# Attention scores of a hybrid encoder block: the keys' low parts by head in full-height tiles, three pools with less in them

## The chip, the cores and the metric

The kernel is one program on one core of a Trainium2 chip. It holds a whole encoder layer, so the attention that is changed here is one stage among several. The metric is the device time of one execution in microseconds (us), the median of several. Engines are named as the profile names them: PE is the TensorE matmul, PEld its weight load, DVE the vector engine, ACT the scalar engine, POOL GpSimd, SP the queue that issues most DMAs.

## The reference, cut to what matters

Mixer B of the layer is attention in chunks of 64 frames: the queries of a chunk see their own chunk and the eight before it, with a bias by clipped distance. There are 8 heads of 64 channels and 1024 frames.

```python
def one_chunk(c):
    qc = q[c*64 : c*64 + 64]                # 64 queries
    kc, vc = kp[...], vp[...]               # 576 keys and values: own chunk and 8 before
    s = einsum('bqhd,bkhd->bhqk', qc, kc) * dh ** -0.5 + bias
    s = where(valid, s, -inf)
    p = softmax(s, axis=-1)
    return einsum('bhqk,bkhd->bqhd', p, vc)
```

Ahead of it stand the RMSNorm, one input projection and mixer A (a gated delta rule); behind it the branch projections with their gates, the output projection, and a feed-forward part with a short convolution.

## The kernel before, in words

**Split operands.** Matmuls run on float32r operands, and precision is kept by splitting a float32 operand into a high part (a rounded copy, made on ACT) and a low part (the rest, a subtraction on DVE or POOL). A product takes two or three matmuls: high by high, low by high, high by low.

**Stages.** In the trace mixer A runs to about 457 us; then come four pairs of attention heads, to about 757 us, then the branch and output projections and the feed-forward part. This case is about the four pairs.

**A pair.** `att_qkv` computes the operands of a pair in half-rows of 512 frames: `proj_half` does 24 matmuls of 512 columns into a PSUM tile `psph` (pool `psP`, two buffers), `scaled` multiplies it by the row scale into `u` on DVE (three buffers), and from `u` come Q, K and V. For head j of the pair, `Q[j]` holds 128 rows: the 64 rows of its own head are the high part of the queries, the other 64 their low part. `Kh[j]` holds the high part of the keys twice, in both halves, so that one matmul of 128 rows gives (query high + query low) by key high. `Kl`, the keys' low part, is one tile for both heads, 64 rows for each. The half-rows of V stay in `u` until `v_half` transposes them on PE into `psvt`.

**A head.** `att_head` goes through 8 query tiles of 128 frames. `scores(t)` makes two products into a PSUM tile `pss` (two buffers):

```python
mm(pss[:, o + s0:o + s1], q, Kh[:, ks], start=True, stop=False)
mm(pss[:, o + s0:o + s1], q[own], Kl[own, ks], start=False, stop=True)
```

The first takes all 128 rows, the second the 64 rows of the head. The band is up to 640 keys, written as pieces of 384 and 256 columns: a tile with t of 4 or more has two pieces and so four matmuls, the four tiles before have one piece (256, 256, 384, 512) and two matmuls. That makes 8 heads x (4 x 4 + 4 x 2) = 192 matmuls, 96 of either product, in 64 score tiles. DVE then adds the bias and takes the row maximum in one pass into `Sb` (four buffers), ACT takes the exponential, DVE scales; `weighted(t)` transposes `Sb` on PE into `psp` and splits it into `PTh` and `PTl`; `values` multiplies them with V into `pso` for every second tile, and the two halves of `pso` are added into `obT` by way of a tile `cor`.

**Order.** `weave` interleaves the turns of `att_pair` (scores run two tiles ahead of their transposes) with the steps of `att_qkv` for the next pair, or with gate projections in the last pair. The tile scheduler then sets the order on each engine by its own estimate, pool buffers included; each engine runs its list in order. So fewer buffers change the order of the program as well as the waits.

Of the kernel before, what the change touches and what calls it, by code (L numbers as in the profile page):

```python
# [8 lines left out]
F32 = mybir.dt.float32  # L9
F32R = mybir.dt.float32r  # L10
AF = mybir.ActivationFunctionType
ALU = mybir.AluOpType
# [4 lines left out]
P = 128  # L17
D = 1024
KT = D // P
T = 1024  # L20
NT = T // P
HN = 512
# [20 lines left out]
BAND = 640  # L43
# [3 lines left out]
def hybrid_kernel(ctx: ExitStack, tc: tile.TileContext, a):  # L47
    nc = tc.nc
    last = {}

    def mm(*args, **kw):
        last["mm"] = nc.tensor.matmul(*args, **kw).ins  # L52
# [591 lines left out]
    c, steps = gdn_qkv(0, ws, lambda e: psc.tile([P, HN], F32, tag="c", name="psph"))  # L644
# [7 lines left out]
    for h in range(-1, GH):  # L652
# [29 lines left out]
        if more:  # L682
            c, steps = gdn_qkv(h + 2)
# [43 lines left out]
    obT = obp2.tile([P, 4, T], F32, name="obT")  # L727
    ax = ExitStack()
    ap_ = ax.enter_context(tc.tile_pool(name="ap", bufs=1, reuse_waits="tile"))
    aq1 = ax.enter_context(tc.tile_pool(name="aq1", bufs=1, reuse_waits="tile"))  # L730
    aqx = ExitStack()
    aq0 = aqx.enter_context(tc.tile_pool(name="aq0", bufs=1, side="right", reuse_waits="tile"))
# [8 lines left out]

    W0 = 4 * GH

    def att_qkv(pr, c):
        c["pr"] = pr
        aq = (aq0, aq1)[pr % 2]
        Q = [aq.tile([P, T], F32R, tag=f"Q{j}", name=f"Q{j}") for j in range(2)]
        Kh = [aq.tile([P, T], F32R, tag=f"Kh{j}", name=f"Kh{j}") for j in range(2)]
        Kl = aq.tile([P, T], F32R, tag="Kl", name="Kl")
        V = aq.tile([P, NT, 256], F32R, tag="V", name="V")  # L750
        Vb = V.bitcast(F32)
        vT = [None, None]

        def scaled(w, e):

            ps, s = proj_half(w, BH, BL, KT, e)
            u = ap_.tile([P, HN], F32, tag="u", name="u", bufs=3)
            nc.vector.tensor_mul(u, ps, rb[:, s])
            return u, s

        def q_half(w, e):
            ps, s = scaled(w, e)
            for j in range(2):
                r = slice(j * 64, (j + 1) * 64)
                x = slice((1 - j) * 64, (2 - j) * 64)
                nc.scalar.activation(Q[j][r, s], ps[r], AF.Copy, scale=0.125)
                nc.vector.scalar_tensor_tensor(out=Q[j][x, s], in0=ps[r], scalar=0.125, in1=Q[j].bitcast(F32)[r, s],
                                               op0=ALU.mult, op1=ALU.subtract)

        def k_half(w, e):  # L770
            ps, s = scaled(w, e)
            for j in range(2):
                r = slice(j * 64, (j + 1) * 64)
                x = slice((1 - j) * 64, (2 - j) * 64)
                nc.scalar.copy(Kh[j][r, s], ps[r])
                nc.scalar.copy(Kh[j][x, s], ps[r])
                nc.vector.tensor_tensor(out=Kl[r, s], in0=ps[r], in1=Kh[j].bitcast(F32)[r, s], op=ALU.subtract)

        def v_half(e):
            ps = psP.tile([P, HN], F32, tag="p", name="psvt")  # L780
            for t in range(4):
                nc.tensor.transpose(out=ps[:, t * P:(t + 1) * P], in_=vT[e][:, t * P:(t + 1) * P],
                                    identity=ident)
            pv = ps.rearrange("p (n j d) -> p n j d", j=2, d=64)
            n = slice(4 * e, 4 * e + 4)
            for j in range(2):
                nc.scalar.copy(V[:, n, j * 192:j * 192 + 64], pv[:, :, j, :])
                nc.vector.tensor_tensor(out=V[:, n, 64 + j * 64:128 + j * 64], in0=pv[:, :, j, :],
                                        in1=Vb[:, n, j * 192:j * 192 + 64], op=ALU.subtract)

        w = load_w(a["w_tiles"][W0 + 8 + pr])
        for e in range(2):
            vT[e], s = scaled(w, e)
            yield
        wq = load_w(a["w_tiles"][W0 + pr])
        wk = load_w(a["w_tiles"][W0 + 4 + pr])
        c.update(Q=Q, Kh=Kh, Kl=Kl, V=V)
        q_half(wq, 0)
        yield
        v_half(0)  # L800
        k_half(wk, 0)
        yield
        v_half(1)
        q_half(wq, 1)
        yield
        k_half(wk, 1)
        yield

    def att_head(c, j):
        pr = c["pr"]  # L810
        h = 2 * pr + j
        Q, Kh, Kl, V = c["Q"][j], c["Kh"][j], c["Kl"], c["V"]
        own = slice(j * 64, (j + 1) * 64)
        bias = ap_.tile([P, BAND], F32, tag="bias", name="bias", bufs=2)
        nc.sync.dma_start(bias, a["rel"][h])
        nc.vector.memset(bias[64:128, 0:64], NEG)
        nc.vector.memset(bias[0:64, BAND - 64:BAND], NEG)

        def scores(t):
            nk = min(t + 1, 5)  # L820
            k0 = t + 1 - nk
            n = nk * P
            o = P if nk == 5 else 0
            pss = psS.tile([P, T], F32, tag="s", name="pss")
            pieces = ((0, 384), (384, 640)) if nk == 5 else ((0, max(n, 256)),)
            q = Q[:, t * P:(t + 1) * P]
            for s0, s1 in pieces:
                ks = slice(k0 * P + s0, k0 * P + s1)
                mm(pss[:, o + s0:o + s1], q, Kh[:, ks], start=True, stop=False)
            for s0, s1 in pieces:  # L830
                ks = slice(k0 * P + s0, k0 * P + s1)
                mm(pss[:, o + s0:o + s1], q[own], Kl[own, ks], start=False, stop=True)
            Sb = ap_.tile([P, BAND], F32, tag="Sb", name="Sb", bufs=4)
            st_ = sml.tile([P, 4], F32, tag="ast", name="ast")
            nc.vector.tensor_tensor_reduce(out=Sb[:, 0:n], in0=pss[:, o:o + n], in1=bias[:, BAND - n:BAND],
                                           scale=1.0, scalar=0.0, op0=ALU.add, op1=ALU.max,
                                           accum_out=st_[:, 0:1])
            nc.vector.tensor_scalar_mul(st_[:, 1:2], st_[:, 0:1], -1.0)
            nc.scalar.activation(Sb[:, 0:n], Sb[:, 0:n], AF.Exp, bias=st_[:, 1:2], accum_out=st_[:, 2:3])
            nc.vector.reciprocal(st_[:, 3:4], st_[:, 2:3])  # L840
            nc.vector.tensor_scalar_mul(Sb[:, 0:n], Sb[:, 0:n], st_[:, 3:4])
            return Sb, nk, k0

        def weighted(t, Sb, nk, k0):
            gq, e = t // 2, t % 2
            ph, pl = PT[gq % 2]
            es = slice(e * P, (e + 1) * P)
            for i0 in range(0, nk, 3):
                m = min(3, nk - i0)
                psp = psT.tile([P, 384], F32, tag="t", name="psp")  # L850
                for i in range(m):
                    nc.tensor.transpose(out=psp[:, i * P:(i + 1) * P], in_=Sb[:, (i0 + i) * P:(i0 + i + 1) * P],  # L852
                                        identity=ident)
                s0 = k0 + i0 - (2 * gq - 4)
                pv = psp[:, 0:m * P].rearrange("p (n q) -> p n q", q=P)
                nc.scalar.copy(ph[:, s0:s0 + m, es], pv)
                nc.vector.tensor_tensor(out=pl[:, s0:s0 + m, es], in0=pv, in1=ph.bitcast(F32)[:, s0:s0 + m, es],
                                        op=ALU.subtract)
        def values(gq):
            ph, pl = PT[gq % 2]  # L860
            f = 6 - min(2 * gq + 2, 6)
            pso = psT.tile([P, 256], F32, tag="t", name="pso")
            for s in range(f, 6):
                v = V[:, 2 * gq - 4 + s, j * P:(j + 1) * P]
                mm(pso, v, ph[:, s, :], start=s == f, stop=False)
                mm(pso, v, pl[:, s, :], start=False, stop=s == 5)
            cor = ap_.tile([P, 256], F32, tag="cor", name="cor")
            oth = slice((1 - j) * 64, (2 - j) * 64)
            nc.scalar.copy(cor[own], pso[oth])
            nc.vector.tensor_add(obT[own, pr, gq * 256:(gq + 1) * 256], pso[own], cor[own])  # L870

        for t in range(NT):
            yield lambda t=t: scores(t), lambda x, t=t: weighted(t, *x), (lambda t=t: values(t // 2)) if t % 2 else None
# [34 lines left out]
    c = {}  # L908
    for _ in att_qkv(0, c):
        pass  # L910
    for pr in range(4):
# [8 lines left out]
        c = nxt  # L920
# [23 lines left out]
    for o in range(KT):  # L944
        wa = load_w(a["w_ba_t"][o])
        wb_ = load_w(a["w_bb_t"][o])
        for e in range(2):
# [4 lines left out]
            ps, s = proj_half(wa, oh, ol, 4, e)  # L952
            nc.vector.scalar_tensor_tensor(out=ta, in0=ta, scalar=1.0, in1=ps, op0=ALU.add, op1=ALU.mult)
            ps, s = proj_half(wb_, bh, bl, 4, e)
# [192 lines left out]
    V, S, G, Q = Pinned(nc.vector), Pinned(nc.scalar), Pinned(nc.gpsimd), Pinned(nc.sync)  # L1147
# [127 lines left out]
    for i, t in enumerate(order):  # L1275
        if t == order[-1]:
            norm_b = norm_operands(order[i - 1], xt, wst, "hi", True)
            next(norm_b)
            o = up_load(0)
# [33 lines left out]
    s, c = slice(T - P, T), slice(HN - P, HN)  # L1313
# [47 lines left out]
    p, r = prs  # L1361
# [429 lines left out]
```

## Time and profile before

| | |
|---|---|
| median of 3 runs | 1605.38 us (1604.98 to 1606.62) |
| profiled execution | 1603.48 us, span of its instructions 1601.4 us |
| PE busy | 1561.8 us, 98% of the span |
| PEld, DVE, ACT, POOL busy | 78%, 70%, 43%, 37% |
| stage of the four pairs, 485 to 757 us | PE 269.35 of 272 us, DVE 194.88 us |

A busy share on PE says that some matmul was under way, not that it was at its pace: matmuls are pipelined, and in the rows below a matmul of 512 columns takes 0.39 us from start to end while the next one starts 0.23 us after it. What a matmul costs is therefore read as the distance from its start to the next start. In the timeline, rows of one kind that follow each other are merged ("x2"), with the start of the first. The column in square brackets is the idle time of the engine ahead of the row and what ended it; "issue" means that the profile shows no one who was waited for.

### The profile page before, as it was taken

To read this page: it belongs to the slowest core of one execution; us is meant where nothing else is said; L and a number is where in the kernel's file an instruction comes from. 1 tells how busy PE (TensorE), PEld (TensorE's weight loads), DVE (VectorE), ACT (ScalarE), POOL (GpSimd) and SP (SyncE) were. 2 spreads that over 40 slices of the span, in tenths; PEclk is the share of its full clock that TensorE was granted. 3 is DMA by queue.
4 is the path that set the end of the run, shared out by engine and by line. 5 is a ranking of instruction groups with operands and counts; after the bars stand their busy time and mean duration, and the time that the engine had idled before them with its cause. 6 is when DMAs were issued, how large, how long until landed. Compare 5 with 4: busy or idle time off the path is not lost.

```text
span 1601.4 us, 21106 instructions
## 1 busy us (share of the span) xinstructions
PE 1561.8 (98%) x7687; PEld 1254.7 (78%) x7687; DVE 1123.8 (70%) x2150; ACT 695.8 (43%) x1376; POOL 589.4 (37%) x445
## 2 busy tenths in 40 slices
PE   8999999999999999999999999999999999999997
PEld 6777776877777777778887887888888888788885
DVE  6795867948436867865665567677777777787787
ACT  7535333352224645554322335444444444333344
POOL 2422212212021101011220248877777776232352
PEclk9999999999999999999999999999999999999998
DMA  7021121122131101111654222233333322775523
GB/s 292 27 81 53 53 73 44 56 61 82 44 122 49 35 23 35 43 53 61 204 171 152 85 93 83 68 111 117 114 114 113 99 99 73 238 247 172 176 92 138
DMA packets 74503, 162.02 MB, mean 101 GB/s; under 512 B 15648, under 2 KB 16928, under 8 KB 74400
## 3 DMA queue, kind: packets, MB, share of 16 engines
q1 hardware_dynamic: 74400, 160.68, 30.2%
q8 instruction: 60, 0.98, 0.3%
q14 instruction: 43, 0.35, 0.1%
HBM read 120.55 MB, written 40.11 MB: 100 GB/s over the span
## 4 chain that ended last, share of the span: by engine, by line
PE 78%; DVE 7%; ACT 2%; issue 1%; DMA 1%; SPq 0%; POOL 0%; POOLq 0%; DVEq 0%; ACTq 0%
PE psph L52 27%; PE psd L52 7%; PE pb L52 7%; PE psout L52 5%; PE pc L52 5%; PE pa L52 4%; PE pb L1131 3%; PE pss L52 3%; PE psd L1483 3%; PE pso L52 3%; PE pc L1131 2%; PE pa L1131 2%; PE psp L852 2%; PE psws L52 1%; DVE tmp L506 1%
## 5 line engine op out<-in xcount | busy, mean ns | idle before, releaser
L82 POOL TENSOR_TENSOR wlo<-wraw,whi 128x1024 fp32r<-128x1024 f32 (+1 forms) x57 | 119.9, 2104 | 481.1 <-ACT whi L81 446.0
L52 PE MATMUL psph<-BH,whi 128*128 128x512 f32 x688 | 281.5, 409 | 9.7 <-ACT BH L220 5.2
L52 PE MATMUL psph<-BL,whi 128*128 128x512 f32 x688 | 278.2, 404 | 0.0
L52 PE MATMUL psph<-BH,wlo 128*128 128x512 f32 x688 | 275.9, 401 | 1.7 <-POOL wlo L82 1.7
L52 PEld LDWEIGHTS psph<-BH,whi 128*128 128x128 f32 x688 | 130.5, 190 | 37.0 <-ACT BH L220 5.9
L1145 POOL TENSOR_TENSOR ol<-wraw,oh 128x512 fp32r<-128x512 f32 x110 | 150.6, 1386 | 9.1 <-ACT oh L1145 9.1
L52 PEld LDWEIGHTS psph<-BH,wlo 128*128 128x128 f32 x688 | 130.5, 190 | 26.5 <-POOL wlo L82 2.1
L52 PEld LDWEIGHTS psph<-BL,whi 128*128 128x128 f32 x688 | 130.3, 189 | 24.5 <-DVE BL L221 1.5
L52 PE MATMUL psd<-wdl,ah 128*128 128x512 f32 (+1 forms) x311 | 121.8, 392 | 5.5 <-DVE wdl L1145 5.5
L1145 POOL TENSOR_TENSOR al<-araw,ah 128x1024 fp32r<-128x1024 f32 (+1 forms) x28 | 68.5, 2447 | 145.3 <-ACT ah L1145 145.2
L1145 POOL TENSOR_TENSOR wraw<-wraw 128x512 f32<-128x512 f32 x86 | 119.4, 1389 | 4.9
L1483 PE MATMUL psd<-wdh,al 128*128 128x512 f32 (+1 forms) x311 | 120.9, 389 | 0.0
L52 PE MATMUL psd<-wdh,ah 128*128 128x512 f32 (+1 forms) x311 | 119.8, 389 | 0.0
L1145 ACT CAST oh<-wraw 128x512 fp32r<-128x512 f32 x110 | 67.6, 619 | 102.0 <-POOL wraw L1145 101.9
L1145 DVE TENSOR_TENSOR wdl<-W,wdh 128x512 fp32r<-128x512 f32 x77 | 88.4, 1186 | 29.4 <-ACT wdh L1145 29.3
L1145 ACT CAST ah<-araw 128x1024 fp32r<-128x1024 f32 (+1 forms) x39 | 40.6, 1040 | 116.7 <-issue 51.9
L81 ACT CAST whi<-wraw 128x1024 fp32r<-128x1024 f32 (+2 forms) x61 | 55.2, 905 | 78.1 <-PE psph L52 54.9
L1145 POOL TENSOR_TENSOR gl<-wraw,gh 128x512 fp32r<-128x512 f32 x42 | 55.8, 1330 | 69.6 <-ACT gh L1145 69.6
L52 PEld LDWEIGHTS psd<-wdl,ah 128*128 128x128 f32 x311 | 58.8, 189 | 20.1 <-DVE wdl L1145 8.1
L1131 PE MATMUL pa<-BH,gh 128*128 128x512 f32 x176 | 68.6, 390 | 0.0
L52 PE MATMUL pa<-BL,gh 128*128 128x512 f32 x176 | 68.5, 389 | 0.0
L52 PE MATMUL pa<-BH,gl 128*128 128x512 f32 x176 | 68.5, 389 | 0.0
(341 smaller groups left out, 3826.1 us busy)
## 6 DMA issues: line engine op xcount, KB each, us to landing
wraw<-w_up SPq DMA_DIRECT2D x44, 512.0 KB, 5.0
wraw<-w_tiles SPq DMA_DIRECT2D x42, 512.0 KB, 3.5
araw<-dA SPq DMA_DIRECT2D x77, 256.0 KB, 3.0
dA<-yu SPq DMA_DIRECT2D x33, 512.0 KB, 3.1
W<-w_down SPq DMA_DIRECT2D x44, 256.0 KB, 4.8
xt<-x SPq DMA_DIRECT2D x16, 512.0 KB, 5.3
dG<-gt SPq DMA_DIRECT2D x16, 512.0 KB, 2.7
ta<-dG SPq DMA_DIRECT2D x16, 256.0 KB, 2.8
```

What stands on the lines that cost most here:

```text
L52: last["mm"] = nc.tensor.matmul(*args, **kw).ins
L81: nc.scalar.copy(hi, src)
L82: (eng or nc.gpsimd).tensor_tensor(out=lo, in0=src, in1=hi.bitcast(F32), op=ALU.subtract)
L506: nc.vector.tensor_tensor(out=tmp[:, :, 0:i], in0=Zt[:, :, 0:i], in1=Lr[:, i:i + 1, 0:i].broadcast_to([P, 8, i]), op=ALU.mult)
L852: nc.tensor.transpose(out=psp[:, i * P:(i + 1) * P], in_=Sb[:, (i0 + i) * P:(i0 + i + 1) * P], identity=ident)
L1131: i = nc.tensor.matmul(ps, wh[:, k], xh[:, k], start=start and k == 0, stop=False, **kw)
L1145: return lambda *args, **kw: tc.keep_in_program_order(f(*args, **kw))
L1483: i = nc.tensor.matmul(ps, al[:, j, ts], wh[:, es], start=False, stop=stop, **kw)
```

## The change

The keys' low parts get a tile for each head, `Kl[j]`, 128 rows high: the 64 rows of the head hold the low part as before, the other 64 hold zeros, written once on POOL into each of the four tiles (two pools of operands, two heads). The second score product then takes all 128 rows of `Q[j]` by all 128 rows of `Kl[j]`. Three edits make room for it: `u` has two buffers instead of three, `Sb` three instead of four, and `cor` is gone, with ACT writing one half of `pso` into `obT` and DVE adding the other half to it in place.

```diff
--- before.py
+++ after.py
@@ -741,12 +741,22 @@
 
     W0 = 4 * GH
 
+    Kls = {}
+
+    def lows(i):
+
+        if i not in Kls:
+            Kls[i] = [(aq0, aq1)[i].tile([P, T], F32R, name=f"Kl{j}") for j in range(2)]
+            for j in range(2):
+                nc.gpsimd.memset(Kls[i][j].bitcast(F32)[(1 - j) * 64:(2 - j) * 64], 0.0)
+        return Kls[i]
+
     def att_qkv(pr, c):
         c["pr"] = pr
         aq = (aq0, aq1)[pr % 2]
         Q = [aq.tile([P, T], F32R, tag=f"Q{j}", name=f"Q{j}") for j in range(2)]
         Kh = [aq.tile([P, T], F32R, tag=f"Kh{j}", name=f"Kh{j}") for j in range(2)]
-        Kl = aq.tile([P, T], F32R, tag="Kl", name="Kl")
+        Kl = lows(pr % 2)
         V = aq.tile([P, NT, 256], F32R, tag="V", name="V")
         Vb = V.bitcast(F32)
         vT = [None, None]
@@ -754,7 +764,7 @@
         def scaled(w, e):
 
             ps, s = proj_half(w, BH, BL, KT, e)
-            u = ap_.tile([P, HN], F32, tag="u", name="u", bufs=3)
+            u = ap_.tile([P, HN], F32, tag="u", name="u", bufs=2)
             nc.vector.tensor_mul(u, ps, rb[:, s])
             return u, s
 
@@ -774,7 +784,7 @@
                 x = slice((1 - j) * 64, (2 - j) * 64)
                 nc.scalar.copy(Kh[j][r, s], ps[r])
                 nc.scalar.copy(Kh[j][x, s], ps[r])
-                nc.vector.tensor_tensor(out=Kl[r, s], in0=ps[r], in1=Kh[j].bitcast(F32)[r, s], op=ALU.subtract)
+                nc.vector.tensor_tensor(out=Kl[j][r, s], in0=ps[r], in1=Kh[j].bitcast(F32)[r, s], op=ALU.subtract)
 
         def v_half(e):
             ps = psP.tile([P, HN], F32, tag="p", name="psvt")
@@ -809,7 +819,7 @@
     def att_head(c, j):
         pr = c["pr"]
         h = 2 * pr + j
-        Q, Kh, Kl, V = c["Q"][j], c["Kh"][j], c["Kl"], c["V"]
+        Q, Kh, Kl, V = c["Q"][j], c["Kh"][j], c["Kl"][j], c["V"]
         own = slice(j * 64, (j + 1) * 64)
         bias = ap_.tile([P, BAND], F32, tag="bias", name="bias", bufs=2)
         nc.sync.dma_start(bias, a["rel"][h])
@@ -829,8 +839,8 @@
                 mm(pss[:, o + s0:o + s1], q, Kh[:, ks], start=True, stop=False)
             for s0, s1 in pieces:
                 ks = slice(k0 * P + s0, k0 * P + s1)
-                mm(pss[:, o + s0:o + s1], q[own], Kl[own, ks], start=False, stop=True)
-            Sb = ap_.tile([P, BAND], F32, tag="Sb", name="Sb", bufs=4)
+                mm(pss[:, o + s0:o + s1], q, Kl[:, ks], start=False, stop=True)
+            Sb = ap_.tile([P, BAND], F32, tag="Sb", name="Sb", bufs=3)
             st_ = sml.tile([P, 4], F32, tag="ast", name="ast")
             nc.vector.tensor_tensor_reduce(out=Sb[:, 0:n], in0=pss[:, o:o + n], in1=bias[:, BAND - n:BAND],
                                            scale=1.0, scalar=0.0, op0=ALU.add, op1=ALU.max,
@@ -864,10 +874,10 @@
                 v = V[:, 2 * gq - 4 + s, j * P:(j + 1) * P]
                 mm(pso, v, ph[:, s, :], start=s == f, stop=False)
                 mm(pso, v, pl[:, s, :], start=False, stop=s == 5)
-            cor = ap_.tile([P, 256], F32, tag="cor", name="cor")
             oth = slice((1 - j) * 64, (2 - j) * 64)
-            nc.scalar.copy(cor[own], pso[oth])
-            nc.vector.tensor_add(obT[own, pr, gq * 256:(gq + 1) * 256], pso[own], cor[own])
+            out = obT[own, pr, gq * 256:(gq + 1) * 256]
+            nc.scalar.copy(out, pso[oth])
+            nc.vector.tensor_add(out, pso[own], out)
 
         for t in range(NT):
             yield lambda t=t: scores(t), lambda x, t=t: weighted(t, *x), (lambda t=t: values(t // 2)) if t % 2 else None
```

In the order of the instructions, the scores keep their matmuls. On PE, the first two score tiles of the first pair, before:

```order
L52 MATMUL psph<-BH,wlo 128x512
L52 MATMUL pss<-Kh_4264,Q_4262 128x256
L52 MATMUL pss<-Kl,Q_4262 128x256
L52 MATMUL pss<-Kh_4264,Q_4262 128x256
L52 MATMUL pss<-Kl,Q_4262 128x256
L52 MATMUL psph<-BH,whi 128x512
```

and now:

```order
L52 MATMUL psph<-BH,wlo 128x512
L52 MATMUL pss<-Kh_4264,Q_4262 128x256
L52 MATMUL pss<-Kl_4266,Q_4262 128x256
L52 MATMUL pss<-Kh_4264,Q_4262 128x256
L52 MATMUL pss<-Kl_4266,Q_4262 128x256
L52 MATMUL psph<-BH,whi 128x512
```

Number, place and columns of the matmuls are the same; the low part has become a tile of the head, and the rows that are contracted (not shown in these rows) go from 64 to 128.

On DVE, where the second head of the first pair begins and the queries' first half of the second pair falls due, before (`ISA Sb` is the pass that adds the bias, `u` the scaled half-row, `Q` the low part of the queries, `PTl` the low part of the transposed weights):

```order
L857 TENSOR_TENSOR PTl_4251<-psp,PTh_4250 128x2x128
L758 TENSOR_TENSOR u<-psph,rb 128x512
L835 ISA Sb,ast<-pss,bias 128x128
L835 ISA ast 128x1
L838 TENSOR_SCALAR ast<-ast 128x1
L857 TENSOR_TENSOR PTl_4257<-psp,PTh_4256 128x3x128
L767 SCALAR_TENSOR_TENSOR Q_4524<-u,Q_4524 64x512
L767 SCALAR_TENSOR_TENSOR Q_4525<-u,Q_4525 64x512
L840 RECIPROCAL ast<-ast 128x1
L857 TENSOR_TENSOR PTl_4257<-psp,PTh_4256 128x2x128
L841 TENSOR_SCALAR Sb<-Sb,ast 128x128
L835 ISA Sb,ast<-pss,bias 128x256
```

and now:

```order
L867 TENSOR_TENSOR PTl_4251<-psp,PTh_4250 128x2x128
L845 ISA Sb,ast<-pss,bias 128x128
L845 ISA ast 128x1
L848 TENSOR_SCALAR ast<-ast 128x1
L867 TENSOR_TENSOR PTl_4257<-psp,PTh_4256 128x3x128
L850 RECIPROCAL ast<-ast 128x1
L845 ISA Sb,ast<-pss,bias 128x256
L845 ISA ast 128x1
L768 TENSOR_TENSOR u<-psph,rb 128x512
L851 TENSOR_SCALAR Sb<-Sb,ast 128x128
L867 TENSOR_TENSOR PTl_4257<-psp,PTh_4256 128x2x128
L848 TENSOR_SCALAR ast<-ast 128x1
```

The write of `u` stands behind two score passes now instead of ahead of them: with two buffers it takes the place of the first half-row of V and has to come after that half-row's transposes on PE. In the first pair, where nothing is interleaved, the order on DVE is as before and the same write waits.

A few rows on, still on DVE, the third score tile of that head (384 columns), before:

```order
L870 TENSOR_TENSOR obT<-pso,cor 64x256
L838 TENSOR_SCALAR ast<-ast 128x1
L835 ISA Sb,ast<-pss,bias 128x384
L835 ISA ast 128x1
L857 TENSOR_TENSOR PTl_4257<-psp,PTh_4256 128x3x128
L840 RECIPROCAL ast<-ast 128x1
L857 TENSOR_TENSOR PTl_4257<-psp,PTh_4256 128x2x128
L841 TENSOR_SCALAR Sb<-Sb,ast 128x256
```

and now:

```order
L880 TENSOR_TENSOR obT<-pso,obT 64x256
L850 RECIPROCAL ast<-ast 128x1
L867 TENSOR_TENSOR PTl_4257<-psp,PTh_4256 128x3x128
L851 TENSOR_SCALAR Sb<-Sb,ast 128x256
L845 ISA Sb,ast<-pss,bias 128x384
L845 ISA ast 128x1
L867 TENSOR_TENSOR PTl_4257<-psp,PTh_4256 128x2x128
L848 TENSOR_SCALAR ast<-ast 128x1
```

With three buffers of `Sb` the third score pass of a head takes the buffer of the last tile of the head before, and has gone behind a `PTl` of that tile. On POOL the four writes of zeros, 64x1024 each, stand together behind the eight small zero fills of `PTh` and `PTl` and ahead of the first `wlo` of the attention.

## Rows read from the trace of the kernel before

**Rows 1.** Page, part 1: busy time of each engine, share, instructions.
```profile
PE 1561.8 (98%) x7687; PEld 1254.7 (78%) x7687; DVE 1123.8 (70%) x2150; ACT 695.8 (43%) x1376; POOL 589.4 (37%) x445
```

**Rows 2.** Windows: window, length, busy of PE, PEld, DVE, ACT, POOL, clock, DMA.
```profile
485.00:757.00 272.00, 269.35 (x1396) 210.92 (x1395) 194.88 (x538) 147.71 (x343) 34.73 (x15) 1.00 0.13 41
```

**Rows 3.** Timeline of PE, a score tile of two pieces: start, length, row.
```profile
636.00 0.39 PE L52 MATMUL psph<-BH,wlo 128*128 128x512 f32 x1
636.23 0.45 PE L52 MATMUL pss<-Kh,Q 128*128 128x384 f32 x2
636.61 0.56 PE L52 MATMUL pss<-Kl,Q 64*128 64x384 f32 x2
637.10 0.66 PE L852 MATMUL psp<-ident,Sb 128*128 128x128 f32 x4
```

**Rows 4.** Timeline of PEld, the weight loads of the same score tile.
```profile
636.00 0.41 PEld L52 LDWEIGHTS pss<-Kh,Q 128*128 128x128 f32 x2
636.61 0.29 PEld L52 LDWEIGHTS pss<-Kl,Q 64*128 64x128 f32 x2 [0.19 <-issue]
637.09 0.42 PEld L852 LDWEIGHTS psp<-ident,Sb 128*128 128x128 f32 x4 [0.19 <-issue]
```

**Rows 5.** Timeline of PE, a score tile of one piece, 384 columns.
```profile
554.40 0.34 PE L52 MATMUL pss<-Kh,Q 128*128 128x384 f32 x1
554.67 0.44 PE L52 MATMUL pss<-Kl,Q 64*128 64x384 f32 x1
555.04 0.50 PE L52 MATMUL psph<-BH,wlo 128*128 128x512 f32 x1
```

**Rows 6.** Waits of PEld, 468 to 760 us: total us, times, longest.
```profile
PEld pss L52 <- issue: 12.7, 56, 0.4
PEld psp L852 <- issue: 6.9, 30, 0.5
```

**Rows 7.** Timeline of PE and DVE, first pair: transposes of V, `u`, next projection.
```profile
479.97 0.60 PE L782 MATMUL psvt<-ident,u 128*128 128x128 f32 x4
480.17 0.69 DVE L758 TENSOR_TENSOR u<-psph,rb 128x512 f32<-128x512 f32 x1 [3.21 <-PE psph L52]
480.92 0.50 PE L52 MATMUL psph<-BH,whi 128*128 128x512 f32 x1 [0.35 <-DVE u L758]
```

**Rows 8.** Timeline of DVE and PE: a queue on DVE ahead of transposes.
```profile
540.62 0.69 DVE L758 TENSOR_TENSOR u<-psph,rb 128x512 f32<-128x512 f32 x1 [0.29 <-PE psph L52]
542.25 2.96 DVE L767 SCALAR_TENSOR_TENSOR Q<-u,Q 64x512 fp32r<-64x512 f32 x2
545.31 0.74 DVE L857 TENSOR_TENSOR PTl<-psp,PTh 128x384 fp32r<-128x384 f32 x2
545.92 0.77 PE L852 MATMUL psp<-ident,Sb 128*128 128x128 f32 x5 [0.62 <-DVE PTl L857]
```

**Rows 9.** The same two engines where the first head begins.
```profile
492.12 0.69 DVE L758 TENSOR_TENSOR u<-psph,rb 128x512 f32<-128x512 f32 x1 [0.84 <-PE psph L52]
497.89 0.33 PE L852 MATMUL psp<-ident,Sb 128*128 128x128 f32 x1 [0.61 <-DVE Sb L841]
```

**Rows 10.** The same, a head's third tile: score pass, older transposes, scaling, own transposes.
```profile
557.15 0.55 DVE L835 CUSTOM_DVE_ANT_0 Sb<-pss,bias 128x384 f32<-128x384 f32 x1
559.01 0.38 PE L852 MATMUL psp<-ident,Sb 128*128 128x128 f32 x2
559.38 0.42 DVE L841 TENSOR_SCALAR Sb<-Sb,ast 128x384 f32<-128x384 f32 x1
566.09 0.55 PE L852 MATMUL psp<-ident,Sb 128*128 128x128 f32 x3
```

**Rows 11.** POOL: zero fills of 1024 columns by form, then a timeline row.
```profile
L352 POOL MEMSET ptA<- 128x1024 f32 x2 | 1.8, 952 | 0.3 <-POOLq L1782 0.3
...
469.09 2.39 POOL L82 TENSOR_TENSOR wlo<-wraw,whi 128x1024 fp32r<-128x1024 f32 x1 [7.65 <-ACT whi L81]
```

## The prediction

> **What bounds the kernel now.** I read the page first: PE is busy for 1561.8 of 1601.4 us, and no other engine is above 78% [rows 1]. A busy PE is not a PE at its pace, so the second view is the stage that the change touches, the windows of 485 to 757 us: PE 269.35 of 272 us, DVE 194.88 us (72%), granted clock 1.00, the upper of the two levels [rows 2]. So the stage lasts as long as PE's list of matmuls lasts at its real pace, and DVE has 77 us to spare in it. The third view is the timeline of PE, read from start to start, since the length of a matmul overlaps with the next.
>
> A matmul of 512 columns holds PE for 0.23 us (636.00 to 636.23) [rows 3]. At that pace 384 columns take 0.17 us and 256 columns 0.12 us, so a product of 640 columns in two pieces should take 0.29 us. The first product of a score tile, 128 rows high, takes 0.38 us (636.23 to 636.61), and the second, 64 rows high, 0.49 us (636.61 to 637.10) [rows 3]. The excess stands around the 64-row matmuls alone: the next start after the 128-row pair is late by 0.09 us, the 64-row pair and the start after it by 0.20 us. The fourth view, PEld, shows why. The two 128-row loads begin at 636.00, together with the matmul ahead of them, and run beside it; the 64-row loads begin only at 636.61, after 0.19 us of idle that no other engine ended, and so does the 128-row load behind them [rows 4]. A load of either height runs hidden under matmuls of its neighbours as long as the height stays 128; at 64 rows, and on the way back, PE stands. A tile of one piece shows the same: 0.27 us and 0.37 us where 0.17 us each would do [rows 5]. This is not rare: the view of waits has 56 such idle stretches ahead of loads for the scores and 30 ahead of the transposes that follow them, 12.7 and 6.9 us [rows 6].
>
> **The second product at full height.** The 96 matmuls of the second product stay, with the same columns; a matmul's time goes by its columns in the rows above, so 64 more rows of zeros cost nothing in it. What goes is the excess: 0.87 us becomes 0.58 us in a two-piece tile [rows 3], and 0.64 us becomes 0.34 us in a one-piece tile [rows 5], so 0.29 to 0.30 us. There are 64 score tiles: 64 x 0.29 = 18.6 us. The trace has no 64-zero-row product, so the bounds: at most the idle of the loads, 12.7 + 6.9 = 19.6 us [rows 6]; at least 0, if the stall hangs on something else than the height. I take 18.6, because the pair `Kh`, `Kh` in the same tile is the wanted case itself: same weights, 128 rows, second load hidden [rows 4].
>
> The rows show 128-row loads running beside 128-row matmuls [rows 4]. [...]
>
> **What is given back.** PE gets nothing where it already waits for DVE, since there DVE's own queue sets the time. Two such places lie behind score tiles.
> - At 545.92 us the transposes waited 0.62 us for `PTl` on DVE. The queue there begins with `u` at 540.62, which waits for a projection that ended ahead of the scores, and runs through two passes for `Q` of 2.96 us together [rows 8]. Three score tiles lie between that projection and the transposes on PE; what they save, 3 x 0.29 = 0.87 us, becomes wait. The place comes back at 609.74 and 673.53, once for each interleaved pair: 3 x 0.87 = 2.6 us.
> - Where the first head begins, the transposes waited 0.61 us for `Sb`, on a chain that begins with `u` at 492.12 and not with the scores [rows 9]. Again three score tiles: 0.9 us.
>
> **Two buffers of `u`.** In a pair the third write of `u` now takes the buffer of the first half-row of V, and the fourth that of the second, so each has to come after four transposes. Today such a write runs beside them: transposes 479.97 to 480.57, `u` from 480.17, and the next projection starts at 480.92 because it waited for `u` [rows 7]. With the wait `u` runs from 480.57 to 481.26 and the projection starts 0.4 us later. In the first pair this happens twice with nothing else for PE to do: 0.8 us. In the pairs behind it the scheduler has put the write behind two score passes, and 12 value matmuls of 256 columns, 12 x 0.12 = 1.4 us, stand between the transposes and the projection; the 0.69 us of `u` hides there. I take 0; without that cover it is 6 x 0.4 = 2.4 us.
>
> **Three buffers of `Sb`.** The third score pass of a head has to wait for the transposes of the last tile of the head before. Today it ran at 557.15, and those transposes at 559.01 to 559.39 [rows 10], so it comes 2.2 us later; behind it on DVE stand `PTl` and the small operations of the softmax, which is why the scheduler moved it. Its scaled result was ready at 559.80 and its own transposes began at 566.09 [rows 10]: 6.3 us of slack hide 2.2. Cost 0; if PE waited for all of it at seven changes of head, 15.4 us.
>
> **Zeros and `cor`.** POOL writes four tiles of 64x1024 zeros. A fill of 1024 columns takes 0.95 us, so 3.8 us, and POOL idles for 7.65 us ahead of the `wlo` behind them [rows 11]: 0, unless two of the fills, which wait for old DMAs, start over 3.8 us late; then each us more is a us of `wlo`. Without `cor` ACT's copy and DVE's add keep their shapes and the copy loses a wait; both are off the path: 0.
>
> **Sum.** -18.6 + 2.6 + 0.9 + 0.8 = -14.3 us. On the profiled execution, 1603.48 us (span 1601.4 and 2.1 around it), that is 1589.2; the median of the runs lies 1.9 us above it, so 1591.1 us.
>
> **Rivals.**
> 1. *DVE hands more back.* Fewer buffers pack the same DVE work into a shorter stage: 195 us in 258 instead of 272, and the 40 us in which heads change are denser than the mean. If the six later writes of `u` lose their cover (2.4 us) and half of the late third passes reach PE (7 x 0.7 = 4.9 us), the time is 1598. For it: the waits of rows 8 and 9 are already of this kind. Against it: 6.3 us of slack [rows 10].
> 2. *The stall stays*, the change then not doing on PE what its shape suggests: the height is not the cause, or full-height loads of these weights are exposed too. Then only the 0.8 us of `u` is left: 1606.2, no change. Against it stand the loads of rows 4.
> 3. *Slower: three `Sb` buffers set the pace.* A buffer is held from the score pass to the end of its transposes, 557.15 to 566.6, some 9.5 us [rows 10]. Three buffers then allow a tile every 3.2 us; the stage needs one every 258 / 64 = 4.0 us. It decides from a hold of 12.1 us on; at 13 us the stage takes 64 x 13 / 3 = 277 us, 19 more than forecast, and the kernel 1610. Against it: PE's filler between scores and transposes is what makes the hold long, and it shrinks when PE is faster.
> 4. *More.* The moved order lets the `PTl` of rows 8 and 9 come earlier, nothing is given back there, and the excess is the 19.6 of rows 6: 1586.
>
> **How the numbers follow.** Forecast 1591.1 with its neighbourhood, 1587 to 1596: 0.70. Rival 1, to 1600: 0.13. Rival 2: 0.06. Rival 3: 0.04. Rival 4: 0.07. What this measurement tells from no change is about 0.2%, 3.2 us. Faster by more: 0.70 + 0.13 + 0.07 = 0.90; the same 0.06; slower 0.04. The range 1586 to 1600 takes in all but rivals 2 and 3.
>
> **What the profile after would show.** Right: `Kl` matmuls as 128x... with about 0.29 us for a pair and 0.17 us for 384 columns, no "issue" idle of PEld ahead of the scores and of what follows; the waits of PE for `PTl` and `Sb` grown to some 1.5 us each at the four places; two starts in the first pair 0.4 us later behind `u`; everything behind the stage only shifted. Wrong: the idle of PEld ahead of `pss` stays near 12.7 us (rival 2); PE waits for `Sb` or `PTl` at every change of head (1); DVE waits for transposes ahead of most score passes (3).

## The result and the profile after

| | before | after | ratio, 95% interval |
|---|---|---|---|
| median, first comparison | 1606.0 us (1604.98 to 1607.79, 4 runs) | 1590.94 us (1590.41 to 1592.53, 4 runs) | 0.9913 [0.9896, 0.9931] |
| median, second comparison | 1605.53 us (17 runs) | 1590.45 us (1588.8 to 1591.5, 4 runs) | 0.9904 [0.9890, 0.9917] |
| profiled execution | 1603.48 us | 1592.53 us | |

The forecast was 1591.1 us. The page's first part and the windows of the stage (columns as in [rows 2]), after:

```profile
PE 1542.7 (97%) x7687; PEld 1255.8 (79%) x7687; DVE 1120.3 (70%) x2150; ACT 698.0 (44%) x1376; POOL 595.6 (37%) x449
```

```profile
485.00:743.00 258.00, 246.99 (x1389) 210.58 (x1388) 193.46 (x537) 147.56 (x341) 33.70 (x14) 1.00 0.13 43
```

The instructions are the same but for the four zero fills. The stage's list of matmuls is done 13.3 us sooner (first to last score matmul 241.3 instead of 254.6 us), and PE now stands idle for 11 of 258 us where it was 2.65 of 272 [rows 2]: part of the gain has turned into waiting.

A score tile of two pieces after the change, PE and PEld in the timeline; these answer to [rows 3] and [rows 4]:

```profile
538.68 0.41 PEld L52 LDWEIGHTS pss<-Kh,Q 128*128 128x128 f32 x2
538.90 0.45 PE L52 MATMUL pss<-Kh,Q 128*128 128x384 f32 x2
539.08 0.31 PEld L52 LDWEIGHTS pss<-Kl,Q 128*128 128x128 f32 x2
539.19 0.46 PE L52 MATMUL pss<-Kl,Q 128*128 128x384 f32 x2
...
539.49 0.60 PE L862 MATMUL psp<-ident,Sb 128*128 128x128 f32 x4
```

From `Kh` to `Kl` 0.29 us (0.38 before), from `Kl` to the next 0.30 us (0.49 before). The loads for `Kl` begin at 539.08, 0.11 us ahead of their matmul, with no idle time in front.

PE's waits in the stage, 485 to 745 us (sum, times, longest):

```profile
PE psp L862 <- DVE PTl L867: 5.7, 5, 1.8
PE psp L862 <- DVE ast L850: 3.2, 3, 1.1
PE psp L862 <- DVE Sb L851: 1.7, 1, 1.7
PE pso L52 <- DVE PTl L867: 0.5, 1, 0.5
```

Before, the first of these was 1.9 us in three waits, the third 0.6 us in one, and the others were not there. The "issue" idle of PEld ahead of the scores, 12.7 us in [rows 6], is gone from the list of its waits. Here are two of the places where PE waits, in the timeline of DVE, POOL and PE. The first answers to [rows 8] and comes three times, as before:

```profile
539.10 0.69 DVE L768 TENSOR_TENSOR u<-psph,rb 128x512 f32<-128x512 f32 x1
...
540.05 2.41 POOL L82 TENSOR_TENSOR wlo<-wraw,whi 128x1024 fp32r<-128x1024 f32 x1 [26.70 <-PE psp L862]
540.57 3.15 DVE L777 SCALAR_TENSOR_TENSOR Q<-u,Q 64x512 fp32r<-64x512 f32 x2
...
544.43 0.76 PE L862 MATMUL psp<-ident,Sb 128*128 128x128 f32 x5 [1.78 <-DVE PTl L867]
...
551.21 0.68 DVE L768 TENSOR_TENSOR u<-psph,rb 128x512 f32<-128x512 f32 x1
...
551.86 2.41 POOL L82 TENSOR_TENSOR wlo<-wraw,whi 128x1024 fp32r<-128x1024 f32 x1 [9.40 <-PE psp L862]
...
552.41 0.55 DVE L867 TENSOR_TENSOR PTl<-psp,PTh 128x384 fp32r<-128x384 f32 x1
...
552.88 1.94 DVE L787 TENSOR_TENSOR Kl<-u,Kh 64x512 fp32r<-64x512 f32 x1
...
554.91 0.69 DVE L787 TENSOR_TENSOR Kl<-u,Kh 64x512 fp32r<-64x512 f32 x1
...
556.26 0.41 PE L862 MATMUL psp<-ident,Sb 128*128 128x128 f32 x2 [1.06 <-DVE ast L850]
```

The second half of this fence, with 1.06 us of wait, is a place that the prediction did not have; it comes three times too. It is again a DVE queue that begins with `u`. In both queues one pass lasts far longer than its like: the first `Kl` takes 1.94 us and the second 0.69, and of the 3.15 us of the two `Q` passes the first takes 2.44. Both long ones end some 0.55 us after the POOL pass beside them has ended (POOL 542.46 and 554.27, DVE 543.01 and 554.82).

The table puts the stage's time into places. It goes through the 1305 matmuls from the first to the last score product and takes the distance from each start to the next. From it, it takes off the pace of undisturbed neighbours, 0.227, 0.170, 0.120 and 0.109 us for 512, 384, 256 and 128 columns (223.65 us in all, in each of these kernels). What is left is the excess, in us; the last three columns are kernels of the next section. A transpose that another kind of matmul follows leaves a negative excess, since the next start comes some 0.03 us after it and not 0.109; these parts are about the same in all columns.

| excess of the stage | before | after | 64 rows again | `wlo` on DVE | gates too |
|---|---|---|---|---|---|
| at the score products, into and out of them | 20.3 | 1.2 | 20.4 | 1.1 | 0.7 |
| at the second start behind them, among transposes or projections | 4.0 | 0.4 | 3.9 | 0.4 | 0.3 |
| ahead of `psp` and `pso`, from other work than scores | 4.1 | 13.7 | 4.5 | 6.5 | 3.3 |
| all the rest | 2.6 | 2.4 | 2.2 | 2.7 | 2.8 |
| all | 31.0 | 17.7 | 31.0 | 10.7 | 7.1 |

### The profile page after: what moved, and what is told of

Its sections match the earlier page's. It is cut to its first block, busy times and chain, and to the rows that moved or that the text cites. A ratio compares the mean times of both kernels' runs of the same rounds, so it can differ in the third digit from the quotient of the medians.

```text
span 1590.6 us, 21158 instructions
## 1 busy us (share of the span) xinstructions
PE 1542.7 (97%) x7687; PEld 1255.8 (79%) x7687; DVE 1120.3 (70%) x2150; ACT 698.0 (44%) x1376; POOL 595.6 (37%) x449
## 4 chain that ended last, share of the span: by engine, by line
PE 49%; DVE 3%; DMA 2%; ACT 1%; issue 1%; SPq 0%; POOL 0%; POOLq 0%; DVEq 0%; ACTq 0%
PE psph L52 8%; PE pb L52 7%; PE psd L52 7%; PE psout L52 5%; PE pc L52 5%; PE pa L52 4%; PE pb L1141 4%; PE psd L1493 3%; PE pc L1141 2%; PE pa L1141 2%; DMA araw<-dA 1%; DVE yu L1155 1%; PE pso L52 0%; DMA oaT<-dO 0%; DVE wdl L1155 0%
```

## The experiments

Theory: the 64-row loads were the stall, and what comes back is DVE's queue behind `u`. Rivals: the smaller pools cost or pay something of their own; the waits are the softmax chain's own length.

**The height alone undone.** The changed kernel, second product on its own rows:

```diff
-                mm(pss[:, o + s0:o + s1], q, Kl[:, ks], start=False, stop=True)
+                mm(pss[:, o + s0:o + s1], q[own], Kl[own, ks], start=False, stop=True)
```

> The changed kernel with one thing undone: the second score product reads its own 64 rows only, as before the change; the two buffers of `u`, the three of `Sb`, the zeros and the order stay. Theory (the height alone pays, and what is handed back to DVE comes only from PE being faster): the excess of about 0.29 us per score tile returns on all 64 tiles, the waits of the transposes at 497.7, 542.3 and 554.8 us shrink to their old 0.6, 0.6 and 0.2 us, and only the 0.4 us of `u` in the first pair is left: 1604.5 to 1607 us, the time of the kernel before. Rival A (fewer buffers cost time of their own): part of the hand-back stays beside the stall, 1608 to 1614 us. Rival B (the fewer buffers and the moved order pay a part of the gain): 1595 to 1602 us.

Measured: 1603.3 us, ratio to before 0.9988 [0.9974, 1.0001]. That is 1.2 us below the range expected and 1.3 us above that of rival B; the profile decides between them. PE's waits in the stage and PEld's wait ahead of the scores:

```profile
PE psp L862 <- DVE PTl L867: 1.9, 3, 0.6
PE psp L862 <- DVE Sb L851: 0.6, 1, 0.6
PE psph L52 <- DVE u L768: 0.3, 1, 0.3
```

```profile
PEld pss L52 <- issue: 12.6, 56, 0.4
```

The first two waits and PEld's are the figures of before (12.7 us in [rows 6]), the third is the wait of [rows 7], which lies inside the window here, and the table's column is nearly that of before, 31.0 us in all. So the height carries the whole gain of the stage, and two buffers of `u`, three of `Sb` and the moved order neither cost nor pay anything in it that can be told. Both rivals on the pools are out. The changed kernel with a buffer more was not run.

**Height or rows of the array.** The kernel before, the second piece's 64-row product on the other half of the rows:

```diff
-                mm(pss[:, o + s0:o + s1], q[own], Kl[own, ks], start=False, stop=True)
+                half = slice((1 - j) * 64, (2 - j) * 64) if s0 else own
+                mm(pss[:, o + s0:o + s1], q[half], Kl[half, ks], start=False, stop=True)
```

> The kernel before, with the second piece's 64-row product on the other 64 rows than the first piece's (it multiplies other data there, so this part of the scores is changed; sizes, loads and columns stay). A rule to test: a weight load runs beside matmuls in flight where the two use different rows. If that rule sets the stall between the two 64-row products of a tile, that stall of 0.11 us goes in 32 tiles, 3.5 us: 1602 to 1603. If the 64-row height itself keeps the load from running ahead, nothing changes: 1605 to 1607, and the second 64-row load of a tile begins no earlier than before.

Measured: 1602.02 us, 0.9986 [0.9973, 0.9998]; the first-to-last time of the scores 252.0 instead of 254.6 us. A two-piece tile, PE and PEld in the timeline:

```profile
636.86 0.19 PEld L52 LDWEIGHTS pss<-Kl,Q 64*128 64x128 f32 x2 [0.19 <-issue]
636.86 0.44 PE L52 MATMUL pss<-Kl,Q 64*128 64x384 f32 x2
637.23 0.31 PEld L853 LDWEIGHTS psp<-ident,Sb 128*128 128x128 f32 x3 [0.18 <-issue]
```

Both loads now begin together (0.19 us for the two, 0.29 in [rows 4]), and the pair takes 0.37 us instead of 0.49: the 0.11 us between the two 64-row products is gone. The idle time on the way in (0.19 us) and out (0.18) is not. At the score products the stage lost 3.5 us of excess (20.3 to 16.8), as the rule on rows asked for, and 1.0 us came back ahead of `psp` and `pso` (4.1 to 5.1). So there were two stalls in such a tile: 0.11 us between two 64-row products in a row on the same rows, and 0.19 and 0.18 us where the height goes from 128 to 64 rows and back. The rule on rows won where the two differed; the height alone was too simple an account of the middle 0.11 us. Why a change of height stalls is not shown.

**Low parts moved to POOL.** In the changed kernel the subtraction for `Kl` on POOL:

```diff
-                nc.vector.tensor_tensor(out=Kl[j][r, s], in0=ps[r], in1=Kh[j].bitcast(F32)[r, s], op=ALU.subtract)
+                nc.gpsimd.tensor_tensor(out=Kl[j][r, s], in0=ps[r], in1=Kh[j].bitcast(F32)[r, s], op=ALU.subtract)
```

> The changed kernel with the subtraction that makes the keys' low parts on POOL instead of DVE. Theory (the waits left are DVE's queue that begins with `u`): the three places like 554.80 us lose most of their 1.06 us wait, and the start at 497.7 us some of its 1.86 us, since two stretched passes of up to 1.9 us leave that queue; 2 to 4 us less than the changed kernel, 1587 to 1589. Rival A (those waits are the softmax chain's own length, not the queue): 1590 to 1592, no change. Rival B (POOL is late with the keys' low parts, behind the weights' low parts of 2.4 us each, and PE waits for `Kl`): 1592 to 1596.

Measured: 1590.92 us, 0.9909 [0.9893, 0.9925], no change. DVE and POOL in the timeline, at the place of the second queue above:

```profile
553.35 2.64 POOL L787 TENSOR_TENSOR Kl<-u,Kh 64x512 fp32r<-64x512 f32 x2
554.01 0.42 DVE L867 TENSOR_TENSOR PTl<-psp,PTh 128x256 fp32r<-128x256 f32 x1 [1.80 <-ACT PTh L866]
...
554.73 1.35 DVE L851 TENSOR_SCALAR Sb<-Sb,ast 128x128 f32<-128x128 f32 x1
```

The `Kl` passes have left the queue, and then DVE waits 1.80 us for ACT (four copies for `Kh` stand ahead of `PTh` there), and a scaling of 128x128, 0.28 us elsewhere, takes 1.35 us while POOL works. That is rival A's time, though not its reason. The start of the first head gained (its wait went from 1.70 to 0.6 us), the place like 544.43 did not (1.8 us again), and the stage lasts 241.6 us, as without the edit (241.3).

**The queries' low part as well.** `Q`'s subtraction on POOL too, the factor 0.125 in the pass that makes `u`:

```diff
-                nc.scalar.activation(Q[j][r, s], ps[r], AF.Copy, scale=0.125)
-                nc.vector.scalar_tensor_tensor(out=Q[j][x, s], in0=ps[r], scalar=0.125, in1=Q[j].bitcast(F32)[r, s],
-                                               op0=ALU.mult, op1=ALU.subtract)
+                nc.scalar.copy(Q[j][r, s], ps[r])
+                nc.gpsimd.tensor_tensor(out=Q[j][x, s], in0=ps[r], in1=Q[j].bitcast(F32)[r, s], op=ALU.subtract)
```

> The one before with the queries' low part on POOL as well; the factor 0.125 goes into the pass on DVE that makes `u`. Theory: the two `Q` passes of 3.15 us together leave the DVE queue of the three places like 542.26 us, whose 1.78 us of wait goes too; 5 to 8 us less than the changed kernel, 1583 to 1586. Rival A (softmax chain, not the queue): 1590 to 1592. Rival B (POOL's list becomes late and PE waits for `Q` or `Kl`): 1592 to 1600.

Measured: 1590.57 us, 0.9907 [0.9890, 0.9924]: 5 to 8 us were expected and none came; the stage lasts 240.7 us instead of 241.3. PE's idle time at 542 us fell from 1.78 to 0.2 us, but 0.7 us at 524 and 1.1 us at 554 stand beside it, three times each. In the queues ahead of these two, scalings again last long beside one of POOL's added passes: 1.04 us for 128x256 at 522.72 and 1.38 us for 128x128 at 552.63. So a queue made shorter this way won next to nothing, and that turned the theory: what POOL does beside DVE's passes may count for more than their number. The run with `wlo` on DVE below tests it.

**The copies for `Kh` shared with DVE.** On top of the last kernel:

```diff
-                nc.scalar.copy(Kh[j][x, s], ps[r])
+                nc.vector.tensor_copy(Kh[j][x, s], ps[r])
```

> The kernel with the queries' and keys' low parts on POOL, and of the four `Kh` copies per half pair on ACT the two duplicates on DVE. With the low parts on POOL, DVE idled 1.75 us ahead of `PTl` at 551.9 us while ACT made four copies of 0.62 us ahead of `PTh`. Theory: that wait was ACT's list, so `PTh` comes 1.2 us earlier, and the transposes behind it wait 1 us less at three places: 1586 to 1589. Rival A (the stretched pass on DVE beside POOL's work sets these places, 1.4 us for a scaling of 128x128): no change, 1589 to 1592.

Measured: 1602.26 us, 0.9983 [0.9970, 0.9995], 10 us above the range of either. POOL, DVE and PE in the timeline:

```profile
554.91 2.39 POOL L82 TENSOR_TENSOR wlo<-wraw,whi 128x1024 fp32r<-128x1024 f32 x1 [4.88 <-PE pss L52]
...
555.21 3.78 DVE L788 CAST Kh<-u 64x512 fp32r<-64x512 f32 x2
...
557.26 2.87 POOL L789 TENSOR_TENSOR Kl<-u,Kh 64x512 fp32r<-64x512 f32 x2
...
559.63 0.39 PE L52 MATMUL pso<-PTh,V 128*128 128x256 f32 x1 [2.86 <-DVE ast L850]
```

Two copies that ACT makes in 0.62 us each hold DVE for 3.78 us, beside two POOL jobs in a row, and PE waits 2.86 us behind them, three times. The first copy, 2.38 us, ends 0.28 us after the `wlo` has. The rival named POOL as the cause, and this timeline speaks for it, but its price was far too small; the copies without POOL beside them were not run.

**POOL taken out of the way.** The changed kernel with the low parts of the attention weights on DVE:

```diff
-        w = load_w(a["w_tiles"][W0 + 8 + pr])
+        w = load_w(a["w_tiles"][W0 + 8 + pr], nc.vector)
-        wq = load_w(a["w_tiles"][W0 + pr])
-        wk = load_w(a["w_tiles"][W0 + 4 + pr])
+        wq = load_w(a["w_tiles"][W0 + pr], nc.vector)
+        wk = load_w(a["w_tiles"][W0 + 4 + pr], nc.vector)
```

> The changed kernel with the low parts of the attention weights (`wlo` of `w`, `wq`, `wk`) on DVE instead of POOL. Theory: `Q` and `Kl` passes on DVE last 1.9 to 3.2 us at the places of the waits because they run beside a POOL pass of 2.4 us; without it a pass of 64x512 takes its 0.69 us, the wait at 554.8 us falls from 1.06 towards 0 and that at 542.3 us from 1.78 to 0.5 or less: 3 x 1 + 3 x 1.3 us, so 6 us less, if the added 1.2 us passes on DVE (about 3 for each of 4 pairs) find idle time of DVE ahead of their use: 1584 to 1587. Rival A (the added passes stand in the same queue and take back what the stretch cost): 1589 to 1593. Rival B (they come late, PE waits for `wlo`): 1593 to 1602.

Measured: 1584.06 us, 0.9868 [0.9855, 0.9881], 6.4 us below the changed kernel, which ran beside it unaltered (1590.45 us, the second comparison of the table above). Its stage lasted 241.3 us again. Of that run was expected:

> The changed kernel unaltered, once more, beside the two below on the same chip. Both theories: 1589 to 1593 us, 0.9890 to 0.9935 of the kernel before; the stage from the first to the last score matmul again about 241 us in the profile.

DVE and POOL of the kernel with `wlo` on DVE in the timeline, at 539 us where POOL is idle and at 654 us where it still makes a low part of the gates' weights:

```profile
539.18 1.40 DVE L777 SCALAR_TENSOR_TENSOR Q<-u,Q 64x512 fp32r<-64x512 f32 x2
...
654.31 2.40 POOL L82 TENSOR_TENSOR wlo<-wraw,whi 128x1024 fp32r<-128x1024 f32 x1 [192.86 <-PE psp L862]
...
654.81 3.16 DVE L777 SCALAR_TENSOR_TENSOR Q<-u,Q 64x512 fp32r<-64x512 f32 x2
```

The same two passes take 1.40 us alone and 3.16 beside POOL, in one kernel. The wait on PE behind the first fell from 1.78 to under 0.2 us, behind the second it stayed at 1.8. The added passes, 1.22 us each, brought no wait of PE for a `wlo` in the stage, and the stage went from 241.3 to 234.3 us.

**The gates' weights too.** On top of the last kernel:

```diff
-        w = load_w(a["w_tiles"][4 * GH + 12 + i])
+        w = load_w(a["w_tiles"][4 * GH + 12 + i], nc.vector)
```

> The kernel with the attention weights' low parts on DVE, and the gates' weights (`gate`, line 167) on DVE as well. In that kernel the wait at 541 us fell to 0.2 us where DVE made the low parts, and stayed at 1.9 us at 656.5 and 1.2 us at 669.1 in the pair where POOL still made a low part of the gates' weights beside `Q` (3.16 us for two passes) and `Kl`. Theory (the stretch beside POOL): both waits fall to about 0.2 us, 2.8 us less in the stage from the first to the last score matmul, 231 to 232 us instead of 234.3; the kernel 1580 to 1582.5. Rival (those two waits are of that pair's own making, or the added passes take it back): 1583.5 to 1586.

Measured: 1572.88 us, 0.9806 [0.9791, 0.9821]: better than either kernel of the case, and 8 us more than the theory asked for. PE's waits in the stage:

```profile
PE psph L52 <- DVE ol L82: 0.7, 1, 0.7
PE psp L862 <- DVE PTl L867: 0.2, 1, 0.2
```

The stage went to 230.7 us; 231 to 232 was expected. The surprise lies ahead of it: the first pair starts 6.8 us earlier (first transposes of V at 468.6 instead of 475.3 us). Gates are computed inside mixer A as well, and one of PE's waits there, for the gate's tile `gt` on DVE, is in the kernel with only the attention weights moved and not in this one:

```profile
PE psph L52 <- DVE gt L171: 3.7, 2, 2.0
```

One group of DVE's passes there, first in that kernel, then in this one (behind the bar: busy us, mean ns of one):

```profile
L506 DVE TENSOR_TENSOR tmp<-Zt,Lr 128x176 f32<-128x176 f32 x4 | 5.4, 1342 | 0.1
```

```profile
L506 DVE TENSOR_TENSOR tmp<-Zt,Lr 128x176 f32<-128x176 f32 x4 | 1.4, 342 | 0.1
```

**The same, without the change.** The kernel before, with the three lines of the attention weights on DVE.

> The kernel before, with nothing but the low parts of the attention weights on DVE. Theory (the stretch of DVE beside POOL is there before the change too, but PE, standing at the 64-row loads, hides nearly all of it): the waits of 0.6 us at the three places go at most, 1603 to 1605.5, that is 0 to 2 us less than before. Rival (moving the low parts is worth 6 to 7 us by itself, whatever the score products do): 1598 to 1600.

Measured: 1602.24 us, 0.9989 [0.9978, 0.9999], 0.8 us below the range of the theory and 2.2 us above that of the rival; the score stage 251.3 instead of 254.6 us, PE's waits there 0.6 us instead of 2.5. So the stretch cost 3.4 us before the change and 7.0 after it (241.3 to 234.3): while PE stood at the 64-row loads, about half of what DVE's lateness costs was covered, and not nearly all of it, as the theory had it.

## Why the prediction came out right, and where its steps were off

**The second product at full height** was the right mechanism and was mis-sized: -18.6 us, and the table shows -19.1 at the score products and another -3.6 at the second start behind them. Both come back when the height alone is undone, so the height is worth 22.6 us; the prediction counted the excess up to the next start only. Its upper bound of 19.6 was too low as well: it took the idle of the loads ahead of the scores and of the transposes [rows 6] and left out that ahead of the projections, which stands in the same view of the kernel before:

```profile
PEld psph L52 <- issue: 3.2, 17, 0.2
```

With it the bound is 22.8 us.

In the traces 128-row loads run beside matmuls on the same 128 rows: in the changed kernel the loads for `Kl` begin at 539.08, while the `Kh` products of 538.90 are under way, to 539.35. Of two 64-row loads in a row the second began 0.11 us behind the first on the same rows [rows 4], and together with it on other rows (636.86). The 0.19 us in and 0.18 out outlived the change of rows.

**What is given back** was the step that failed in size: 2.6 + 0.9 us forecast, 9.6 measured (4.1 to 13.7 in the table). Of this the start of the first head made 1.1 us ([rows 9]: 0.61 of wait, now 1.70), the three places like [rows 8] 1.15 each (0.62, now 1.78), 0.2 to 0.3 us above the forecast. What it lacked were three places like 556.26, 1.0 us more each, and some 2 us in smaller ones, the largest 0.5 us in the last pair. The rule that it used holds at 556.26 too: a DVE queue that begins with `u`, and three score tiles on PE between. These places had almost no wait before, so the list of waits did not show them; slack that is nearly used up is not in a list of waits. And the prediction took the 2.96 us for `Q` as given, where `u`, twice as high, took 0.69 [rows 8]. That difference is the stretch beside POOL (in the kernel before the first of the two passes began at 542.25, with POOL in a subtraction to 543.95, and took 2.24 us, the second 0.69), and the start of the first head has it too, in POOL and DVE of the changed kernel:

```profile
494.94 2.40 POOL L82 TENSOR_TENSOR wlo<-wraw,whi 128x1024 fp32r<-128x1024 f32 x1 [3.05 <-ACT whi L81]
495.41 2.47 DVE L787 TENSOR_TENSOR Kl<-u,Kh 64x512 fp32r<-64x512 f32 x1
```

Taking POOL's attention passes away took 7.0 us off the stage.

**Two buffers of `u`**: 0.8 forecast, 0.4 measured. At the first place the projection waited 0.87 us for `u`, where it had waited 0.44 us for ACT before. At the second it waited 0.35 us, as before: `u` began at 482.03, ahead of the end of the transposes beside it (482.43), so it did not take the buffer of the second half-row of V, as the prediction had it, but one that had come free. The first place, PE and DVE in the timeline; it answers to [rows 7]:

```profile
474.83 0.60 PE L792 MATMUL psvt<-ident,u 128*128 128x128 f32 x4
...
475.46 0.69 DVE L768 TENSOR_TENSOR u<-psph,rb 128x512 f32<-128x512 f32 x1 [5.19 <-PE psvt L792]
...
476.30 0.47 PE L52 MATMUL psph<-BH,whi 128*128 128x512 f32 x1 [0.87 <-DVE u L768]
```

**Three buffers of `Sb`** and **zeros**: 0, as forecast. The third tile's pass came 1.05 us later, though PE was 1.9 us further on there (the transposes of 558.19 us before came at 556.26), so it moved some 3 us against PE, 2.2 forecast. Its transposes came 3.2 us after its scaling had ended, 6.3 before [rows 10]: half of the slack is used, and the cost is 0. The fills ran ahead of the `wlo` with 3.65 us to spare. DVE and PE, then POOL, in the timeline:

```profile
558.20 0.56 DVE L845 CUSTOM_DVE_ANT_0 Sb<-pss,bias 128x384 f32<-128x384 f32 x1
...
560.14 0.42 DVE L851 TENSOR_SCALAR Sb<-Sb,ast 128x384 f32<-128x384 f32 x1
...
563.79 0.38 PE L862 MATMUL psp<-ident,Sb 128*128 128x128 f32 x2
```

```profile
462.93 3.96 POOL L751 MEMSET Kl<- 64x1024 f32 x4
470.55 2.39 POOL L82 TENSOR_TENSOR wlo<-wraw,whi 128x1024 fp32r<-128x1024 f32 x1 [3.65 <-ACT whi L81]
```

**The sum** was -14.3 and came to -22.6 + 9.6 + 0.4 = -12.6 us, or -12.9 with the -0.3 of the table's other places (-13.3 from the first to the last score matmul, and 0.4 ahead of it). Two errors of 4.0 and 6.1 us against each other made the total look better than its terms, and that the forecast lies within 0.2 us of the median is luck. The profiled executions differ by 11.0 us and the medians by 15.1. Between the stage and the profiled executions stand some 1.5 us of the granted clock: in the changed kernel's execution it fell once more than in that of the kernel before, from 1.00 to 0.50, the only two values in the traces of the two, for 3.4 us of mixer A, in code that is not changed, and the first transposes of V came 1.46 us later (474.83, 473.37 before). In the 3 us ahead of that fall PE was busy for 1.74 us; in the kernel before it was busy for 1.84 us there and the clock stayed at 1.00. Two windows of that stretch, with the columns of [rows 2]:

```profile
374.00:375.00 1.00, 1.00 (x4) 0.33 (x2) 0.83 (x4) 0.00 (x0) 0.00 (x0) 0.50 0.82 319
375.00:376.00 1.00, 1.00 (x4) 0.78 (x4) 0.17 (x1) 0.00 (x0) 0.00 (x0) 0.50 0.30 119
```

The other 2 to 3 us, between the stage and the medians, lie in executions that have no profile, and stay open.

**The rivals.** Rival 1 named the right engine and the wrong places: PE's waits have none for `u` in later pairs, and the third score pass cost nothing. Rivals 2, 3 and 4 did not happen.

## What to carry to other kernels

Where a matmul of half the rows stands between full-height ones, look at the weight loads: here filling the rows with zeros cost nothing in columns (0.30 us for the two full-height products of a tile, 0.29 by the pace of the table) and took the stalls on both sides away, 22.6 us. Before you credit a faster stage, list the queues of the other engines that begin with a result made ahead of it, those without a wait today too, since they can set the new end. And where a pass takes two to three times its usual length, as `Kl` here with 1.94 us instead of 0.69, look at what runs beside it before you move or split it: here taking POOL's passes out of DVE's way, those of the gates' weights included, gave as much again as the change itself (0.9904 of the time before with the change, 0.9806 with both).

## What the runs showed of the hardware

Some DVE passes that read and write SBUF alone ended only after a POOL subtraction that they had begun in. In the changed kernel these are four of the 16 `Kl` passes and four of the 16 `Q` passes: they ended 0.54 to 0.55 us after POOL's and took 1.92 to 2.47 us and 2.43 to 2.45 us, the other twelve of each 0.68 to 0.69. `Kl` from 64x512 took 1.94 us when it began at 552.88 with POOL busy to 554.27. Two `tmp` passes of 128x176 took 2.12 and 2.55 us, the other two 0.34; the scalings of `Sb` (1.04 us for 128x256, 1.35 and 1.38 us for 128x128) and the copies for `Kh` above (3.78 us for two) are of this kind. Not every pass on SBUF alone is held: a reduction of 128x256 in mixer A took 0.42 us in the middle of a POOL subtraction, in the timeline of POOL and DVE of the changed kernel,

```profile
399.81 2.60 POOL L82 TENSOR_TENSOR wlo<-wraw,whi 128x1024 fp32r<-128x1024 f32 x1 [9.40 <-ACT whi L81]
...
400.18 0.42 DVE L508 TENSOR_REDUCE Zt<-tmp 128x8 f32<-128x256 f32 x1
```

and the eight scalings of `ast` (L848), one column wide, that began in one took 0.14 to 0.16 us, as the others did. The `PTl` passes, which read PSUM, took no longer beside POOL: `PTl` at 552.41, inside the same POOL pass as `Kl`, took 0.55 us, its mean in the stage (554 ns over 47), and the ten of 128x384 that began in a POOL subtraction 0.55 to 0.56. Why some passes are held and others are not is not shown.

Two 64-row products on different halves of the rows, 0.44 and 0.38 us long, are shown within 0.44 us (from 636.86), yet it is 0.37 us from there to the next start, against 0.30 us for two full-height ones after each other (539.19 to 539.49).
